# A two-layer diffusion trunk: twelve modulation vectors as row sums, spread over the whole program

## The chip, the cores and the metric

The kernel runs on one core of a Trainium2 chip. TensorE (PE) multiplies, VectorE (DVE), ScalarE (ACT) and GpSimd (POOL) work on rows of 128 partitions, and SyncE (SP) issues most transfers. Each engine takes its instructions in the order in which they are written, and waits on semaphores of the others. The metric is the device time in microseconds (us), lower is better.

## The reference, cut to what matters

```python
for l in range(2):                                 # two layers, same weights for context and latent tokens
    mods = split(silu(cond) @ w_ada[l] + b_ada[l], 9)      # shift, scale, gate of three norms; 1024 each
    x += 0.5 * gt1 * swiglu(rms_norm(x, g0) * (1 + sc1) + sh1)      # ffn1, 1024 -> 2*2816 -> 1024
    u = rms_norm(x, g1) * (1 + sc2) + sh2
    z = u @ w_in                                   # 1024 -> 4112: attention, Fourier, mLSTM, gates
    x += gt2 * ((sum over 3 branches of sigmoid(u @ w_gate_b) * (branch_b @ w_br_b)) @ w_out)
    x += 0.5 * gt3 * swiglu(rms_norm(x, g2) * (1 + sc3) + sh3)      # ffn2
y = rms_norm(x, g_final)
```

There are 128 context and 128 latent tokens, so 256 columns. Everything is float32. `cond` is one vector for the context tokens and one for the latent ones, so that each of the 9 modulations of a layer is a product of a 1024 x 1024 matrix with two columns.

## The kernel before, in words

The tokens lie as columns: `xT` holds 8 blocks of 128 channels by 256 tokens. The products take a float32 weight as two parts, a rounded high half (`whi`, cast on ACT) and the rest (`wlo`, subtracted on DVE); activations are split the same way (`uh`, `ul`), and `mm3` does three products for each pair. A weight arrives by DMA in chunks of up to 1 MB into one of 6 `raw` buffers, is split in units of 128 x 1024 elements by `split_one`, and up to 6 units may be split and not yet used up.

The program is a list of steps. `add` appends a step with its function and the units that it needs; the last loop walks over the list, calls each function, and behind most steps `pump_split` splits further units while fewer than 6 are live. The order of that walk is the order of each engine's queue. A unit that isn't split (`split=False`) is read straight from `raw`.

A layer is FFN 1, mixer and FFN 2. An FFN has an input stage (11 pairs of 4 units of 24 products, `silu` times gate) and an output stage (4 pairs of output blocks, 3 units for each block, then `residual` adds into `xT`). The mixer projects `w_in`, and then runs three branches with their gates; pieces of attention and of the recurrence (`lanes`) are run between and within its steps. `w_out` ends it. In the attention, DVE makes `pc` (the difference of two softmaxes) and PE transposes it.

Layer 0 starts with `begin`: in 9 slices PE makes the first shift and scale (`ada`, one block of 128 channels each), `channel` turns it into `uh`, `ul`, and `products` runs three FFN pairs, each slab of whose weights is one channel block deep. Three pairs of PSUM tiles are evicted at its end by `done`.

The other 16 modulations (the dictionary `ADA`) are made either on DVE (first list of an entry: a product with the condition `cb` along rows of the transposed weights `w_adaT`, with the sum kept; 16 of these sums make one modulation) or on PE (second list: raw weights against `cT`, in two groups of 16 products each, copied to `adaev` and transposed at the end). `mod_steps` writes both, and `spread_into` spreads them evenly over a stage: the whole FFN input stage or the mixer's branches.

Of the kernel before, what the change touches and what calls it, by code (L numbers as in the profile page):

```python
# [116 lines left out]
class Step:  # L117
    def __init__(self, fn, units=(), pump=True, lanes=False, ahead=()):
        self.fn, self.units, self.pump, self.lanes = fn, list(units), pump, lanes
        self.ahead = list(ahead)  # L120


@with_exitstack
def trunk_kernel(ctx: ExitStack, tc: tile.TileContext, a: dict):
# [94 lines left out]
    run = {"lanes": False}  # L219
    late, held = [], []  # L220

    def add(fn, units=(), pump=True, ln=False, ahead=()):
        steps.append(Step(fn, units, pump, ln, ahead))

    def pump_lanes(which=(0, 1, 2)):
# [69 lines left out]


    def mod_steps(mods_):

        on_ve, mods_ = mods_
        st = {"left": 4 * len(mods_)}
        seq = []

# [10 lines left out]

        def finish(l, m, o, x):
            bT = parT[l][:, m * KD:(m + 1) * KD].unsqueeze(2).to_broadcast([P, KD, 2])
            ve.tensor_add(o, x, bT)  # L320
            if m % 3 == 1:
                k0 = 72 + m // 3 * KD
                gT = parT[l][:, k0:k0 + KD].unsqueeze(2).to_broadcast([P, KD, 2])
                ve.scalar_tensor_tensor(o, o, 1.0, gT, op0=ALU.add, op1=ALU.mult)
            elif m % 3 == 2 and m != 5:
                ve.tensor_scalar(o, o, 0.5, None, op0=ALU.mult)

        for i, (l, m) in enumerate(on_ve):
            o, junk = mods[l, m], []
            for j in range(KD // 2):  # L330
                ch = Chunk(a["w_adaT"][l, m, j], 2, D)
                for b in range(2):
                    for g in range(2):
                        u = Unit(ch, b, b + 1, 0, D, split=False)

                        def fn(u=u, k=2 * j + b, g=g, o=o, l=l, m=m, junk=junk):
                            if not junk:
                                junk.append(blk([P, D], "junkw"))
                            ve.tensor_tensor_reduce(junk[0], u.raw()[:, 0, :], cb[:, g, :], 1.0, 0.0,  # L339
                                                    op0=ALU.mult, op1=ALU.add, accum_out=o[:, k, g:g + 1])  # L340
                            if k == KD - 1 and g == 1:
                                finish(l, m, o, o)

                        seq.append(((i + (4 * j + 2 * b + g) / 16) / len(on_ve), fn, [u]))
        for i, (l, m) in enumerate(mods_):
            for j2 in range(2):
                us = []
                for j in range(2 * j2, 2 * j2 + 2):
                    ch = Chunk(a["w_ada"][l, j * 256:(j + 1) * 256, m * D:(m + 1) * D], 2, D)
                    us.append(Unit(ch, 0, 2, 0, D, split=False))  # L350

                def fn(us=us, i=i, j2=j2):
                    for j, u in enumerate(us, 2 * j2):
                        raw = u.raw().rearrange("p e (r c f) -> p e c r f", r=2, c=2)
                        side([(cT[:, 2 * j + e, CT - 2 * i:CT - 2 * i + 32], raw[:, e, c])
                              for e in range(2) for c in range(2)], 0, 512)

                seq.append(((2 * i + j2 + 0.4) / (2 * len(mods_)), fn, us))
        seq.sort(key=lambda x: x[0])
        out = [x[1:] for x in seq]  # L360
        if not mods_:
            return out

        def post():
# [12 lines left out]
            for i, (l, m) in enumerate(mods_):  # L377
                finish(l, m, mods[l, m], full[:, :, 2 * i:2 * i + 2])

        out.append((post, []))  # L380
# [174 lines left out]

    def residual(k, ps, gate, norm):
        for g in range(2):
# [25 lines left out]
    def add_ffn(l, which, norm, norm_next, mods_, begun=None):  # L583
        w_out = a[f"w_ffn{which}_out"][l]
        gate = mods[l, 2 if which == 1 else 8]
        hT = {}

# [28 lines left out]
        n_pair = NF // 2  # L616
        p0 = len(steps)
        for jj in range(n_pair):
            if jj == FIRST + 1 and l == 0 and which == 1:
                add(s_params2)  # L620
            if jj == 0:
                if begun is not None:
# [4 lines left out]
            elif begun is None or jj >= FIRST:  # L627
                us, st = ffn_units(l, which, jj), {}
                for nm, i in (("a", 0), ("a", 1), ("g", 0), ("g", 1)):
# [12 lines left out]
                    add(fn, [us[2 * i + (nm == "g")]])  # L642
        p1 = len(steps)

        ks = [(0, 8), (8, 16), (16, 22)]
        for mp in range(4):
            ps = [None, None]
            for k0, k1 in ks:
                ch = Chunk(w_out[k0 * P:k1 * P, mp * 256:(mp + 1) * 256], k1 - k0, 256)
                for i in range(2):  # L650
# [3 lines left out]
                    def fn(u=u, i=i, m=m, ps=ps, k0=k0, k1=k1):  # L654
# [6 lines left out]
                        if k1 == NF:  # L661
                            residual(m, ps[i], gate, norm_next)

                    add(fn, [u], pump=not (mp == 3 and k1 == NF))
        spread_into(p0 + (14 if begun else 0), p1, mods_)


    def add_mixer(l, norm, norm_next, mods_):
# [522 lines left out]

        us = b8_units(w_in, 0) + b8_units(w_in, 256)
        add(lambda: first(norm, us, q_done), us, pump=2)
        add(loads2, pump=False)
        bform("k", 512)
        aform("v", 1024, v_tile)
        steps.insert(len(steps) - 3, Step(gates))
# [6 lines left out]

        p0 = len(steps) + 6
        mg = {}
        wb = {0: a["w_br_attn"][l], 1: a["w_br_four"][l], 2: a["w_br_mlstm"][l]}
        wg = a["w_branch_gate"][l]
        for bi, br in enumerate(BRANCHES):
            for mq in range(2):  # L1210
# [14 lines left out]
                if mq == 0:  # L1225
                    def drain(br=br):
                        while not M.get(f"ok{br}") and pump_lanes():
                            pass
                    add(drain)

                for p in range(2):
                    def fb(u=Unit(chb, 0, 4, p * 256, p * 256 + 256), st=sts[p], p=p, mq=mq, bi=bi, br=br):
# [30 lines left out]

        gate = mods[l, 5]
        for mp in range(4):
            us_ = b8_units(a["w_out"][l], mp * 256)
            if mp == 0:
                def fn(us_=us_):
# [6 lines left out]
                    for m in range(2):  # L1275
                        residual(m, ps[m], gate, norm_next)
                add(fn, us_)
                continue
            for i in range(2):
                def fn(u=us_[i], m=2 * mp + i):  # L1280
                    p_ = pm([P, 256])
                    prod8(p_, u, mk_)
                    residual(m, p_, gate, norm_next)
                add(fn, [us_[i]], pump=mp < 3)
        spread_into(p0, len(steps) - 8, mods_)
        return loads
# [16 lines left out]
    def begin(done):  # L1303
# [5 lines left out]
        win = a["w_ffn1_in"][0]  # L1309
        ev, ps, v = {}, [], []  # L1310
        b1 = tmp([P, KD], "b1", bufs=1)
# [21 lines left out]
        def channel(k):  # L1333
# [26 lines left out]
        def slice_(j, u, us):  # L1360
            if j < KD:
                ada(j, u)
            if j == 0:
# [41 lines left out]
    for l in range(DEPTH):  # L1405
        add_ffn(l, 1, norms[l, 0], norms[l, 1], ADA[l, "ffn1"], begin if l == 0 else None)
        pos = len(steps)
        steps.insert(pos - 6, Step(add_mixer(l, norms[l, 1], norms[l, 2], ADA[l, "mixer"]), pump=False))
        add_ffn(l, 2, norms[l, 2], norms[l + 1, 0], ADA[l, "ffn2"])

# [17 lines left out]

    add(fin)


# [113 lines left out]
```

## Time and profile before

| | us |
|---|---|
| median of three runs | 1352.44 (1351.43 to 1352.7) |
| the profiled execution | 1352.04 |
| its span, first to last instruction | 1350.3 |
| PE, DVE, ACT, POOL busy in the span | 1325.8, 961.0, 683.5, 112.4 |

The execution's own time is 1.7 us longer than its span. Busy time is time in which at least one instruction of the engine runs; an engine that is always busy need not be the one that sets the time, so waits are read beside it.

### The profile page before, as it was taken

Reading aid. Unit: us, or ns where it says so; the run is one execution under the profiler, and the core shown is the slowest. Engines: PE = TensorE matmul, PEld = TensorE weight load, DVE = VectorE, ACT = ScalarE, POOL = GpSimd, SP = SyncE. Lnnn points to the kernel's source line nnn. Section 1 sums busy time; section 2 is a strip of 40 time slices with the busy share of each in tenths; the row PEclk is TensorE's granted clock in tenths of the full one; section 3 lists DMA queues with packets and bytes.
Section 4 is the critical chain, followed back from the end, with each engine's and each line's share of the span. In section 5 each row is a group of like instructions: output and inputs, shape, how many; then the busy total and the mean of one; then the engine's idle time right before and its main releaser. Section 6 shows DMA issues by size and latency. Waiting matters only on the chain.

```text
span 1350.3 us, 25902 instructions
## 1 busy us (share of the span) xinstructions
PE 1325.8 (98%) x10748; PEld 1257.2 (93%) x10748; DVE 961.0 (71%) x1535; ACT 683.5 (51%) x1097; POOL 112.4 (8%) x136
## 2 busy tenths in 40 slices
PE   8999999999999999999999999999999999999998
PEld 5899999788989998999999999998899899999998
DVE  4699866775557689977669976677565668886653
ACT  4564445665644465444455444456654445654441
POOL 2000003100000040000120000130000001200001
PEclk9999999999999999999999999999999999999999
DMA  9999864754588638987639886747446895477630
GB/s 366 339 342 320 289 191 148 219 183 129 172 287 304 221 126 282 312 303 234 197 125 304 305 297 201 200 146 218 132 152 226 294 303 163 153 259 236 216 100 32
DMA packets 220565, 304.72 MB, mean 226 GB/s; under 512 B 5584, under 2 KB 190176, under 8 KB 215712
## 3 DMA queue, kind: packets, MB, share of 16 engines
q1 hardware_dynamic: 216320, 295.93, 65.8%
q0 software_dynamic: 1680, 5.05, 1.1%
q10 hardware_dynamic: 2448, 2.10, 0.6%
q8 instruction: 84, 1.38, 0.4%
q14 instruction: 33, 0.27, 0.1%
HBM read 298.85 MB, written 3.15 MB: 224 GB/s over the span
## 4 chain that ended last, share of the span: by engine, by line
PE 83%; DVE 9%; ACT 3%; DMA 3%; issue 2%; ACTq 0%; POOL 0%; SPq 0%; DVEq 0%
PE pm L167 24%; PE pm L169 24%; PE pm L168 24%; PE pd L164 3%; DVE wlo L1474 3%; PE pb L164 2%; ACT whi L1473 2%; DVE v L488 2%; DMA raw<-w_ada 2%; DVE ul L179 1%; DVE junkw L339 1%; PE pa L164 1%; PE pm L736 1%; PE pm L738 1%; PE pm L737 1%
## 5 line engine op out<-in xcount | busy, mean ns | idle before, releaser
L1474 DVE TENSOR_TENSOR wlo<-raw,whi 128x1024 fp32r<-128x1024 f32 (+1 forms) x428 | 508.9, 1195 | 282.9 <-ACT whi L1473 275.2
L1473 ACT CAST whi<-raw 128x1024 fp32r<-128x1024 f32 (+1 forms) x428 | 434.9, 1025 | 336.3 <-PE pm L168 242.2
L167 PE MATMUL pm<-uh,whi 128*128 128x256 f32 x1904 | 545.2, 286 | 1.9 <-ACT uh L178 1.0
L169 PE MATMUL pm<-uh,wlo 128*128 128x256 f32 x1904 | 536.0, 282 | 4.9 <-DVE wlo L1474 4.9
L168 PE MATMUL pm<-ul,whi 128*128 128x256 f32 x1904 | 536.5, 282 | 1.8 <-DVE v L488 1.3
L167 PEld LDWEIGHTS pm<-uh,whi 128*128 128x128 f32 x1904 | 360.5, 189 | 20.9 <-issue 8.8
L169 PEld LDWEIGHTS pm<-uh,wlo 128*128 128x128 f32 x1904 | 358.8, 188 | 6.4 <-DVE wlo L1474 6.3
L168 PEld LDWEIGHTS pm<-ul,whi 128*128 128x128 f32 x1904 | 359.8, 189 | 4.3 <-DVE ul L179 1.9
L169 PE MATMUL pm<-hh,wlo 128*128 128x256 f32 x704 | 198.3, 282 | 0.0
L168 PE MATMUL pm<-hl,whi 128*128 128x256 f32 x704 | 197.8, 281 | 0.0
L167 PE MATMUL pm<-hh,whi 128*128 128x256 f32 x704 | 197.6, 281 | 0.0
L339 DVE CUSTOM_DVE_ANT_0 junkw<-raw,cb 128x1024 f32<-128x1024 f32 x112 | 136.5, 1219 | 0.1
L167 PEld LDWEIGHTS pm<-hh,whi 128*128 128x128 f32 x704 | 132.8, 189 | 0.0
L168 PEld LDWEIGHTS pm<-hl,whi 128*128 128x128 f32 x704 | 132.7, 188 | 0.0
L169 PEld LDWEIGHTS pm<-hh,wlo 128*128 128x128 f32 x704 | 132.5, 188 | 0.0
L413 POOL TENSOR_TENSOR nsum<-nsum,nsq 128x256 f32<-128x256 f32 x36 | 36.4, 1011 | 806.5 <-ACT nsq L411 806.5
L637 ACT ACTIVATE silu<-pm 128x512 f32<-128x512 f32 x38 | 22.7, 597 | 53.1 <-PE pm L169 53.1
L164 PE MATMUL pd<-raw,cT 128*32 128x512 f32 (+1 forms) x416 | 43.8, 533 | 4.9 <-DMA raw<-w_ada 4.9
L178 ACT CAST hh<-silu 128x512 fp32r<-128x512 f32 x41 | 25.3, 621 | 37.6 <-DVE silu L639 37.6
L558 DVE SCALAR_TENSOR_TENSOR xT<-pm,mod,xT 128x128 f32<-128x128 f32 x96 | 28.8, 342 | 17.9 <-PE pm L169 17.8
L1222 ACT ACTIVATE sig<-pm 128x512 f32<-128x512 f32 x24 | 14.4, 598 | 49.9 <-PE pm L169 49.8
L736 PE MATMUL pm<-whi,uh 128*128 128x512 f32 x96 | 39.3, 410 | 0.0
(337 smaller groups left out, 1755.5 us busy)
## 6 DMA issues: line engine op xcount, KB each, us to landing
raw<-w_ffn_in SPq DMA_DIRECT2D x82, 1024.0 KB, 7.1
raw<-w_ada SPq DMA_DIRECT2D x44, 1024.0 KB, 5.6
raw<-w_ffn_out SPq DMA_DIRECT2D x32, 1024.0 KB, 5.6
raw<-w_in SPq DMA_DIRECT2D x32, 1024.0 KB, 5.8
raw<-w_adaT SPq DMA_DIRECT2D x28, 1024.0 KB, 6.5
raw<-w_branch_gate SPq DMA_DIRECT2D x24, 1024.0 KB, 5.3
raw<-w_ffn_out SPq DMA_DIRECT2D x16, 768.0 KB, 4.6
raw<-w_out SPq DMA_DIRECT2D x8, 1024.0 KB, 6.3
```

The costliest lines, as they stand in the source:

```text
L164: pe.matmul(out, lhsT, rhs, start=start, stop=stop)
L167: pe.matmul(out, sh, mh, start=start, stop=False)
L168: pe.matmul(out, sh, ml, start=False, stop=False)
L169: pe.matmul(out, sl, mh, start=False, stop=stop)
L178: ac.copy(hi, src)
L339: ve.tensor_tensor_reduce(junk[0], u.raw()[:, 0, :], cb[:, g, :], 1.0, 0.0, op0=ALU.mult, op1=ALU.add, accum_out=o[:, k, g:g + 1])
L413: eng.tensor_add(self.sum, self.sum, sq)
L488: ve.tensor_scalar(v[:, G[1]], v[:, G[1]], self.scale[:, k, 1:2], self.shift[:, k, 1:2], op0=ALU.mult, op1=ALU.add)
L558: ve.scalar_tensor_tensor(xT[:, k, G[g]], ps[:, G[g]], gate[:, k, g:g + 1], xT[:, k, G[g]], op0=ALU.mult, op1=ALU.add)
L736: pe.matmul(ps[g], xh[:, G[g]], wh, start=(k == 0), stop=False)
L1473: ac.copy(u.hi, r)
L1474: ve.tensor_sub(u.lo, r, u.hi.bitcast(F32))
```

## The change

Of the 16 modulations behind `begin`, 12 are now row sums on DVE instead of 7, and 4 stay on PE instead of 9 (`ADA`, one for each of four stages). The 192 row sums (12 times 16) stand in one list in the order of `ROWS`, and no longer belong to a stage: each step of the program has a rate (`RATE`: 0.93 or 0.85 for a step of an FFN's input stage, 0.75 in the output stage except its last quarter, 0.3 in the mixer's projections, 0.35 and 0.5 in its branches, 0 elsewhere), and whenever the rates of the steps passed add up to one, the next sum is put behind that step. The product that a sum leaves behind goes to one bf16 tile, `junkw`, instead of a float32 block.

In `begin`, POOL no longer multiplies `xT` by the norm's factor ahead of the channels; each channel now does that with its scale in two DVE operations, adds the shift in the cast on ACT, and subtracts in two more DVE operations. In the first slice, the channel comes ahead of both splits of the slab. In the last slice, one split stands ahead of each of the three evictions.

```diff
-CT = 8
-
-ADA = {(0, "ffn1"): ([(0, 4), (0, 3)], [(0, 2)]),
-       (0, "mixer"): ([], [(0, 7), (0, 6), (0, 5)]),
-       (0, "ffn2"): ([(1, 1), (1, 0)], [(0, 8)]),
-       (1, "ffn1"): ([(1, 4), (1, 3)], [(1, 2)]),
-       (1, "mixer"): ([], [(1, 7), (1, 6), (1, 5)]),
-       (1, "ffn2"): ([(1, 8)], [])}
+CT = 0
+
+ADA = {(0, "ffn1"): [(0, 2)], (0, "mixer"): [(0, 5)], (0, "ffn2"): [(0, 8)], (1, "mixer"): [(1, 5)]}
+ROWS = [(0, 4), (0, 3), (0, 7), (0, 6), (1, 1), (1, 0), (1, 2), (1, 4), (1, 3), (1, 7), (1, 6), (1, 8)]
+
+RATE = {"in0": 0.93, "in": 0.85, "out": 0.75, "win": 0.3, "branch": 0.35, "last": 0.5, "merge": 0.0}
...
+    junkw = const.tile([P, D], BF16, name="junkw")
...
+    def row_steps():
+
+        for l, m in ROWS:
+            o = mods[l, m]
+            for j in range(KD // 2):
+                ch = Chunk(a["w_adaT"][l, m, j], 2, D)
+                for b in range(2):
+                    for g in range(2):
+                        u = Unit(ch, b, b + 1, 0, D, split=False)
+
+                        def fn(u=u, k=2 * j + b, g=g, o=o, l=l, m=m):
+                            ve.tensor_tensor_reduce(junkw, u.raw()[:, 0, :], cb[:, g, :], 1.0, 0.0,
+                                                    op0=ALU.mult, op1=ALU.add, accum_out=o[:, k, g:g + 1])
+                            if k == KD - 1 and g == 1:
+                                finish(l, m, o, o)
+                                known.add((l, m))
+
+                        yield fn, [u]
...
-            i, r = k // 4, k % 4
-            x = v[i][:, r, :]
-            ac.activation(x[:, G[0]], x[:, G[0]], AF.Identity, scale=sc[:, 0:1], bias=sh[:, 0:1])
-            ve.tensor_scalar(x[:, G[1]], x[:, G[1]], sc[:, 1:2], sh[:, 1:2], op0=ALU.mult, op1=ALU.add)
-            hilo(x, U.h[i][:, r, :], U.l[i][:, r, :])
+            x = t2([P, 256], "v0")
+            xh, xl = uk(k)
+            for g in range(2):
+                ve.scalar_tensor_tensor(x[:, G[g]], xT[:, k, G[g]], sc[:, g:g + 1], norm.bc[:, G[g]],
+                                        op0=ALU.mult, op1=ALU.mult)
+            for g in range(2):
+                ac.activation(xh[:, G[g]], x[:, G[g]], AF.Identity, bias=sh[:, g:g + 1])
+            for g in range(2):
+                ve.scalar_tensor_tensor(xl[:, G[g]], x[:, G[g]], sh[:, g:g + 1], xh[:, G[g]].bitcast(F32),
+                                        op0=ALU.add, op1=ALU.subtract)
...
-                for i in range(2):
-                    v.append(blk([P, 4, 256], f"v{i}"))
-                    for r in range(4):
-                        (po if i or r else ve).tensor_mul(v[i][:, r, :], xT[:, 4 * i + r, :], norm.bc)
...
             if j < KD:
-                split_one()
+                if j:
+                    split_one()
                 channel(j)
-                split_one()
+                while st["unit"] < 2 * j + 2:
+                    split_one()
             else:
+                pump_split(1)
                 done(0, ps[0])
             for i in range(1, FIRST):
                 if j:
                     products(j - 1, i, us)
                 if j == KD:
+                    pump_split(1)
                     done(i, ps[i])
...
+    todo, due = row_steps(), 0.0
+    for s in steps:
+        s.slot = []
+        due += s.rate
+        while due >= 1.0:
+            due -= 1.0
+            nxt = next(todo, None)
+            if nxt is not None:
+                s.slot.append(Step(*nxt))
+    steps[:] = [x for s in steps for x in (s, *s.slot)]
```

Three places of DVE's queue show what moves. The first is the first channel of `begin`; `mo` is the channel's modulation as summed from PSUM, `v` the normed block. Before:

```order
L1373 TENSOR_TENSOR v_213<-xT,bcs 128x256
L1474 TENSOR_TENSOR wlo<-raw_122,whi 128x768
L1340 TENSOR_REDUCE mo_230<-pd 128x4
L1343 SCALAR_TENSOR_TENSOR mod_1_97<-mo_230,b_119,parT_94 128x2
L1344 TENSOR_SCALAR mod_0_96<-mo_230,parT_94 128x2
L1348 TENSOR_SCALAR v_213<-v_213,mod_1_97,mod_0_96 128x128
L179 TENSOR_TENSOR ul_201<-v_213,uh_199 128x256
L1474 TENSOR_TENSOR wlo<-raw_122,whi 128x768
```

And in the changed kernel, where the slab's two splits (`wlo`) come behind the channel:

```order
L1359 TENSOR_REDUCE mo_217<-pd 128x4
L1362 SCALAR_TENSOR_TENSOR mod_1_97<-mo_217,b_120,parT_94 128x2
L1363 TENSOR_SCALAR mod_0_96<-mo_217,parT_94 128x2
L1367 SCALAR_TENSOR_TENSOR v_221<-xT,mod_1_97,bcs 128x128 x2
L1372 SCALAR_TENSOR_TENSOR ul_202<-v_221,mod_0_96,uh_200 128x128 x2
L1510 TENSOR_TENSOR wlo<-raw_123,whi 128x768 x2
```

The second place is the output stage of layer 0's first FFN, the first unit of `w_out` behind two residuals (`xT`), before:

```order
L558 SCALAR_TENSOR_TENSOR xT<-pm,mod_2_98,xT 128x128 x2
L1474 TENSOR_TENSOR wlo<-raw_1790,whi 128x768
L426 TENSOR_SCALAR y<-xT,mod_4_100 128x128
L179 TENSOR_TENSOR yl_2083<-y,yh_2081 128x256
L1474 TENSOR_TENSOR wlo<-raw_1855,whi 128x1024 x2
L1474 TENSOR_TENSOR wlo<-raw_1859,whi 128x1024 x2
L558 SCALAR_TENSOR_TENSOR xT<-pm,mod_2_98,xT 128x128 x2
```

And now, where `junkw` marks a row sum (the row behind it reads the sum out):

```order
L559 SCALAR_TENSOR_TENSOR xT<-pm,mod_2_98,xT 128x128 x2
L1510 TENSOR_TENSOR wlo<-raw_1877,whi 128x768
L426 TENSOR_SCALAR y<-xT,mod_4_100 128x128
L178 TENSOR_TENSOR yl_2097<-y,yh_2095 128x256
L319 ISA junkw,mod_7_103<-raw_1874,cb 128x1024
L319 ISA mod_7_103 128x1
L1510 TENSOR_TENSOR wlo<-raw_1940,whi 128x1024 x2
L319 ISA junkw,mod_7_103<-raw_1874,cb 128x1024
L319 ISA mod_7_103 128x1
L1510 TENSOR_TENSOR wlo<-raw_2004,whi 128x1024
```

Between two residuals stand four or five sums that were not there. Counted over the program, the output stages of the four FFNs now hold 19, 18, 19 and 0 sums (4, 3, 3 and 2 before), the input stages 25, 29, 29 and 11 (28, 29, 29 and 14 before), each mixer 21 (none before).

The third place is the mixer of layer 0, from the row maxima `mx` of the attention scores to `pc`. The rows on `gpk` are the gates of the recurrence. Before:

```order
L1474 TENSOR_TENSOR wlo<-raw_2847,whi 128x1024 x2
L835 TENSOR_REDUCE mx<-pa 128x4 x2
...
L1474 TENSOR_TENSOR wlo<-raw_2892,whi 128x1024
L844 RECIPROCAL rs<-sm 128x8
L846 TENSOR_TENSOR cf<-sm,rs 128x4
L847 TENSOR_SCALAR cf<-cf,lamn 128x4
L849 SCALAR_TENSOR_TENSOR pc<-e_3192,cf,pc 128x128 x4
```

And now, with one sum between the two splits ahead of `mx` and one behind the last split ahead of `pc`:

```order
L1510 TENSOR_TENSOR wlo<-raw_2878,whi 128x1024
L319 ISA junkw,mod_7_103<-raw_2888,cb 128x1024
L319 ISA mod_7_103 128x1
L1510 TENSOR_TENSOR wlo<-raw_2878,whi 128x1024
L845 TENSOR_REDUCE mx<-pa 128x4 x2
...
L1510 TENSOR_TENSOR wlo<-raw_3003,whi 128x1024
L319 ISA junkw,mod_7_103<-raw_2888,cb 128x1024
L319 ISA mod_7_103 128x1
L854 RECIPROCAL rs<-sm 128x8
L856 TENSOR_TENSOR cf<-sm,rs 128x4
L857 TENSOR_SCALAR cf<-cf,lamn 128x4
L859 SCALAR_TENSOR_TENSOR pc<-e_3224,cf,pc 128x128 x4
```

In layer 1 two sums stand in the same stretch, the second one split earlier.

## Rows read from the trace of the kernel before

**Rows 1.** The page's busy time (share of the span) and instructions of each engine.

```profile
PE 1325.8 (98%) x10748; PEld 1257.2 (93%) x10748; DVE 961.0 (71%) x1535; ACT 683.5 (51%) x1097; POOL 112.4 (8%) x136
```

**Rows 2.** The list of waits: who waited for whom, us in total, times, longest.

```profile
ACT whi L1473 <- PE pm L168: 242.2, 165, 4.3
...
PE pm L169 <- DVE wlo L1474: 4.9, 7, 0.8
```

**Rows 3.** PE's timeline around one group: start, us, operation, count.

```profile
129.22 0.28 PE L169 MATMUL pm<-uh,wlo 128*128 128x256 f32 x1
129.43 1.92 PE L164 MATMUL pd<-raw,cT 128*32 128x512 f32 x16
131.28 0.39 PE L167 MATMUL pm<-uh,whi 128*128 128x256 f32 x1
131.51 0.28 PE L168 MATMUL pm<-ul,whi 128*128 128x256 f32 x1
```

**Rows 4.** PE's timeline at a closing step of layer 1's mixer.

```profile
1112.76 0.60 PE L172 MATMUL pd<-cst,adaev 128*128 128x128 f32 x4
1113.11 0.36 PE L167 MATMUL pm<-uh,whi 128*128 128x256 f32 x1
```

**Rows 5.** PE's timeline in FFN 1 of layer 1, and PE's waits from 60 us.

```profile
725.65 1.07 PE L164 MATMUL pd<-raw,cT 128*32 128x512 f32 x8 [1.41 <-DMA raw<-w_ada]
...
PE pd L164 <- DMA raw<-w_ada: 2.7, 3, 1.4
```

**Rows 6.** PE's timeline at the end of the opening, idle time before it in brackets.

```profile
63.01 0.38 PE L167 MATMUL pm<-uh,whi 128*128 128x256 f32 x1 [0.91 <-ACT whi L1473]
...
64.27 0.39 PE L169 MATMUL pm<-uh,wlo 128*128 128x256 f32 x1 [0.76 <-DVE wlo L1474]
```

**Rows 7.** PE's timeline around the first slab's products.

```profile
14.30 1.07 PE L164 MATMUL pd<-raw,cT 128*32 128x256 f32 x16 [1.16 <-DMA raw<-w_ada]
16.41 0.38 PE L167 MATMUL pm<-uh,whi 128*128 128x256 f32 x1 [1.04 <-ACT uh L178]
18.28 0.39 PE L169 MATMUL pm<-uh,wlo 128*128 128x256 f32 x1 [0.32 <-DVE wlo L1474]
```

**Rows 8.** DVE's timeline in the first channel and in the second.

```profile
12.73 1.09 DVE L1474 TENSOR_TENSOR wlo<-raw,whi 128x768 fp32r<-128x768 f32 x1 [0.31 <-ACT whi L1473]
...
14.34 0.78 DVE L1344 TENSOR_SCALAR mod<-mo,parT 128x2 f32<-128x2 f32 x1
15.16 0.70 DVE L1348 TENSOR_SCALAR v<-v,mod,mod 128x128 f32<-128x128 f32 x1
...
20.08 0.22 DVE L1344 TENSOR_SCALAR mod<-mo,parT 128x2 f32<-128x2 f32 x1
20.41 0.34 DVE L1348 TENSOR_SCALAR v<-v,mod,mod 128x128 f32<-128x128 f32 x1
```

**Rows 9.** POOL's timeline in the first slice.

```profile
12.04 6.79 POOL L1373 TENSOR_TENSOR v<-xT,bcs 128x256 f32<-128x256 f32 x7 [2.02 <-ACT bcs L476]
```

**Rows 10.** Four stretches: length, busy PE, PEld, DVE, ACT, POOL, clock, DMA.

```profile
18.40:22.00 3.60, 3.60 (x18) 3.60 (x19) 2.55 (x6) 1.57 (x3) 0.43 (x1) 0.53 1.03 419
28.00:34.00 6.00, 6.00 (x59) 5.28 (x58) 3.13 (x7) 3.04 (x7) 0.00 (x0) 1.00 0.93 341
157.00:222.00 65.00, 65.00 (x550) 65.00 (x549) 39.88 (x64) 29.93 (x43) 5.75 (x6) 1.00 0.66 204
260.00:440.00 180.00, 178.39 (x1363) 160.27 (x1362) 113.06 (x195) 95.78 (x189) 8.79 (x11) 1.00 0.64 214
```

**Rows 11.** DVE's timeline at the first row sum, with what follows it.

```profile
73.20 1.22 DVE L339 CUSTOM_DVE_ANT_0 junkw<-raw,cb 128x1024 f32<-128x1024 f32 x1
74.34 0.09 DVE L339 DVE_READ_ACCUMULATOR2_ANT mod<- 128x1 f32 x1
74.34 1.22 DVE L1474 TENSOR_TENSOR wlo<-raw,whi 128x1024 fp32r<-128x1024 f32 x1
```

**Rows 12.** The mixer of layer 0: DVE's timeline, and PE's transposes of `pc`.

```profile
270.57 1.23 DVE L1474 TENSOR_TENSOR wlo<-raw,whi 128x1024 fp32r<-128x1024 f32 x1 [0.90 <-ACT whi L1473]
...
282.53 1.14 DVE L849 SCALAR_TENSOR_TENSOR pc<-e,cf,pc 128x128 f32<-128x128 f32 x4
...
282.94 1.11 PE L172 MATMUL pa<-cst,pc 128*128 128x128 f32 x4 [0.52 <-DVE pc L849]
```

More of the change, by code (lines that the diff above doesn't have):

```diff
@@ L120, in __init__ @@
         self.ahead = list(ahead)
+        self.rate = 0.0
 @with_exitstack
@@ L218, in trunk_kernel @@
     lanes = [[], [], []]
-    run = {"lanes": False}
+    run = {"lanes": False, "rate": 0.0}
     late, held = [], []
@@ L223, in add @@
         steps.append(Step(fn, units, pump, ln, ahead))
+        steps[-1].rate = run["rate"]
     def pump_lanes(which=(0, 1, 2)):
@@ L294, in x_in, with finish @@
                 (ac.copy if g and not k4 else ve.tensor_copy)(xT[:, 4 * k4:4 * k4 + 4, G[g]], t)
+    def finish(l, m, o, x):
+        bT = parT[l][:, m * KD:(m + 1) * KD].unsqueeze(2).to_broadcast([P, KD, 2])
+        ve.tensor_add(o, x, bT)
+        if m % 3 == 1:
+            k0 = 72 + m // 3 * KD
+            gT = parT[l][:, k0:k0 + KD].unsqueeze(2).to_broadcast([P, KD, 2])
+            ve.scalar_tensor_tensor(o, o, 1.0, gT, op0=ALU.add, op1=ALU.mult)
+        elif m % 3 == 2 and m != 5:
+            ve.tensor_scalar(o, o, 0.5, None, op0=ALU.mult)
+    def row_steps():
[13 more added lines that the diff above has]
+                        yield fn, [u]
+    known = set()
     def mod_steps(mods_):
-        on_ve, mods_ = mods_
         st = {"left": 4 * len(mods_)}
-        seq = []
+        out = []
         def side(tiles, f0, f1):
@@ L316, in side @@
                 ac.copy(st["ev"], st["ps"])
[L318 to L344, printed above, removed]
         for i, (l, m) in enumerate(mods_):
@@ L356, in fn @@
                               for e in range(2) for c in range(2)], 0, 512)
[L358 to L362, printed above, removed]
+                out.append((fn, us))
         def post():
@@ L378, in post @@
                 finish(l, m, mods[l, m], full[:, :, 2 * i:2 * i + 2])
+                known.add((l, m))
         out.append((post, []))
@@ L554, in prod8, with residual @@
                 mid()
-    def residual(k, ps, gate, norm):
+    def residual(k, ps, gate, norm, of):
+        assert of <= known, (of, known)
         for g in range(2):
@@ L585, in add_ffn @@
         gate = mods[l, 2 if which == 1 else 8]
+        of = {(l, 2), (l, 3), (l, 4)} if which == 1 else {(l, 8), (l + 1, 0), (l + 1, 1)}
+        of = {x for x in of if x[0] < DEPTH}
         hT = {}
@@ L617, in add_ffn @@
         p0 = len(steps)
+        run["rate"] = 0.0
         for jj in range(n_pair):
@@ L620, in add_ffn @@
                 add(s_params2)
+            if jj == (FIRST if begun else 1):
+                run["rate"] = RATE["in0" if begun else "in"]
             if jj == 0:
@@ L643, in add_ffn @@
         p1 = len(steps)
+        run["rate"] = RATE["out"]
         ks = [(0, 8), (8, 16), (16, 22)]
@@ L647, in add_ffn @@
             ps = [None, None]
+            if mp == 3:
+                run["rate"] = 0.0
             for k0, k1 in ks:
@@ L661, in fn @@
                         if k1 == NF:
-                            residual(m, ps[i], gate, norm_next)
+                            residual(m, ps[i], gate, norm_next, of)
                     add(fn, [u], pump=not (mp == 3 and k1 == NF))
-        spread_into(p0 + (14 if begun else 0), p1, mods_)
+        if mods_:
+            spread_into(p0 + (14 if begun else 0), p1, mods_)
     def add_mixer(l, norm, norm_next, mods_):
@@ L1192, in add_mixer @@
         us = b8_units(w_in, 0) + b8_units(w_in, 256)
+        run["rate"] = 0.0
         add(lambda: first(norm, us, q_done), us, pump=2)
@@ L1195, in add_mixer @@
         bform("k", 512)
+        run["rate"] = RATE["win"]
         aform("v", 1024, v_tile)
@@ L1205, in add_mixer @@
         p0 = len(steps) + 6
+        run["rate"] = RATE["branch"]
         mg = {}
@@ L1228, in drain @@
                             pass
+                    if bi == 2:
+                        run["rate"] = RATE["last"]
                     add(drain)
+                if bi == 2 and mq == 1:
+                    run["rate"] = 0.0
                 for p in range(2):
@@ L1262, in mk_ @@
             return mg["h", k // 4][:, k % 4, :], mg["l", k // 4][:, k % 4, :]
-        gate = mods[l, 5]
+        gate, of = mods[l, 5], {(l, 5), (l, 6), (l, 7)}
         for mp in range(4):
             us_ = b8_units(a["w_out"][l], mp * 256)
+            run["rate"] = RATE["merge"] if mp in (1, 2) else 0.0
             if mp == 0:
@@ L1275, in fn @@
                     for m in range(2):
-                        residual(m, ps[m], gate, norm_next)
+                        residual(m, ps[m], gate, norm_next, of)
                 add(fn, us_)
@@ L1282, in fn @@
                     prod8(p_, u, mk_)
-                    residual(m, p_, gate, norm_next)
+                    residual(m, p_, gate, norm_next, of)
                 add(fn, [us_[i]], pump=mp < 3)
-        spread_into(p0, len(steps) - 8, mods_)
+        if mods_:
+            spread_into(p0, len(steps) - 8, mods_)
         return loads
@@ L1429, in trunk_kernel @@
     add(fin)
+    todo, due = row_steps(), 0.0
[8 more added lines that the diff above has]
+    steps[:] = [x for s in steps for x in (s, *s.slot)]
+    assert next(todo, None) is None
     units, need, floor = [], {}, 0
```

8 lines of the change are left out of this document (4 added, 4 removed).

## The prediction

> **What bounds the kernel now.** I read the page's busy table first: TensorE (PE) is busy in 98% of the 1350.3 us span, VectorE (DVE) in 71%, ScalarE (ACT) in 51% [rows 1]. A busy PE need not be the bound, so the list of waits comes next. The reader should see its direction: ACT waits 242.2 us for PE to give back a buffer of split weights, and PE waits only 4.9 us for the low halves that DVE makes [rows 2]. So the two engines that prepare the weights run their full six splits ahead nearly all the time, and PE sets the pace. What leaves PE's queue shortens the program; what is added on DVE costs nothing as long as DVE keeps its lead, and what it delays is not a thing that PE takes next.
>
> **The change, part by part**
>
> *Five modulations leave PE.* Each has two groups of 16 products. Around one group, product starts stand 129.22 to 131.28, and the next gap is 0.23 where 0.12 is usual [rows 3]. So a group costs 2.06 - 0.12 + 0.11 = 2.05 us; ten groups: 20.5 us. One closing step of five goes as well: four transposes of 0.60 us in the trace's busy time, but the next product starts 0.35 us after them [rows 4]; I take 0.4. Nothing hides either: PE's rows touch on both sides.
>
> *Waits for the weights of those groups.* The stall before the second half of the group at 723 us is 1.41 us, and this group is gone; three such stalls sum to 2.7 us [rows 5]. The other two belong to groups that stay but move; 0 to 1.3 us, I take half, 0.6. Together 2.0.
>
> *Splits amid the first evictions.* After the nine-step opening PE idles 0.91 us for the first high half and 0.76 us for its low half [rows 6], because ACT and DVE evict three pairs before they split. Now a split stands before each eviction, some 3 us ahead of PE's need. Gain 0 to 1.67; I take 1.7. Later evictions are the price: the PSUM buffers that they free are next written by PE after the pair that it is then on, so one split's delay is hidden.
>
> *First channel.* The second half of the first slab is waited for until 18.28 us; the first product had waited until 16.41, behind a group that itself waited for its DMA until 14.30 [rows 7]. In the DVE queue a split of 1.09 us stands ahead of the channel's small operations, and two of these take 0.78 and 0.70 us where the next channel takes 0.22 and 0.34, while POOL runs its products [rows 8, 9]. Now the split comes behind, and POOL is idle: 1.09 + 0.56 + 0.36 = 2.0 us earlier. The DMA limits it: if PE ran straight on from 14.30 + 1.07 = 15.37, the ninth product would start at 15.37 + 8 x 0.12 = 16.3 instead of 18.28. I take 1.9; bounds 0 and 2.0. Each channel's DVE work becomes four short two-input operations in place of one and a subtraction; this is hidden under PE's own slice, in which DVE is busy 3.13 us of 6 [rows 10]. If the clock's slow stretch behind it, 3.60 us at 0.53 (the lower level) [rows 10], also went, up to 1.5 us more would be gained; PE still stops for the same DMA before it, so I count 0.
>
> *Eighty more row sums on DVE.* One takes 1.22 us, and the next operation starts 1.14 us after it, the read of the sum lying beside it [rows 11]. In the three FFN output stages 19, 18 and 19 stand where 4, 3 and 3 stood, in the two mixers 21 each where none stood; the FFN input stages have 6 fewer and the last output stage 2. The first output stage keeps DVE busy 39.88 of 65 us [rows 10], its few old sums included; 15 more make 39.9 + 17.1 = 57.0. It fits, with a lead of six splits before it and none of the sums in its last quarter, so 0. The mixer of layer 0 keeps DVE busy 113 of 180 us [rows 10], and 21 sums add 24. Room again, but here order matters: two sums now stand ahead of the attention operation that writes `pc`, and PE waits for just this one already, 0.52 us at 282.94 [rows 12]. The first sum falls partly into the 0.90 us for which DVE idles at 270.57; the second falls into a stretch without a gap [rows 12]. So `pc` comes 0.24 + 1.14 = 1.4 us later, and PE with it; the same in layer 1: -2.8 us. Bounds 0 and two full sums, 4.6. What is queued behind on DVE (gate rows, a split) has waited for other things than PE. For the other 38 mixer sums the trace shows no PE wait that they would lengthen; each could cost nothing or up to 1.14 us. I take 1.0 us for all, nearest to a stretch in which PE has hardly any idle.
>
> Does a sum really cost 1.22 us in its new place? It writes bf16 now, and no such sum ran before; the copied-out product is never read, and every sum before took two f32 inputs at the pace of a plain subtraction of equal length, 1.22 us [rows 11].
> [...]
>
> Sum: 20.5 + 0.4 + 2.0 + 1.7 + 1.9 - 2.8 - 1.0 = 22.7 us. The profiled execution took 1352.04 us, 1.7 more than its span; the median of the runs is 1352.44. From the former 1329.3, from the latter 1329.7, which I give.
>
> **The rivals**
>
> 1. *The sums reach PE.* If one in four of the other 38 mixer sums stood before something that PE takes next, and each output stage lost one sum's length at its end, 10 x 1.14 + 3 x 1.14 = 15 us would be lost, less the 1.0 already counted: 1343. For it: two of 42 clearly do. Against it: DVE idle before most splits, ACT's long waits for PE.
> 2. *The gain runs into the lead.* PE, relieved, catches up with the splits and waits there: if half of the 20.5 came back, 1340. Against it: 242.2 us of ACT waiting for PE, some twelve times what is removed.
> 3. *Slower: the mixer's chain.* The attention and recurrence operations pass from PE to DVE and back; if most mixer sums stood in that chain, up to 38 x 1.14 = 43 us would be lost, at the full count 1329.7 + 42 = 1372. It decides from 21 of the 38 on (23.7 us against 22.7 + 1.0). Against it: PE waited for DVE in this chain only at `pc`.
> 4. *Dearer sums.* The output stage has (65 - 39.9)/15 = 1.67 us for each added sum; at twice the measured length, 2.44 us, it would overrun by 11.6 us, and three of them bring 35 us: 1365, slower. The measured 1.22 leaves it little chance. [...]
> 5. *Better.* `pc` and the other mixer sums cost nothing, the slow-clock stretch and all DMA stalls go: 1329.7 - 2.8 - 1.0 - 1.5 - 0.7 = 1323.7.
>
> **How the numbers follow.** Chances: forecast (1325 to 1336) 0.66, rival 1 0.18, rival 2 0.05, rival 3 0.03, rival 4 0.02, better 0.06. A measurement of this kernel tells about 0.2%, some 2.7 us, from no change. The range goes from 1322, just past the better case, to 1339, which cuts off most of rivals 1 and 2, 3 and 4: 0.8 are inside. Faster 0.94 (all but rivals 3, 4 and a sliver of 1), within 0.2% 0.02, slower 0.04.
>
> **What would show it.** Right: PE busy near 1301 us; about 21 us fewer PE products; no gap at 62 us; first slab's ninth product near 16.4; PE's wait for `pc` near 1.9 us in each mixer; row sums of 1.22 us; ACT still waiting over 200 us for PE. Wrong: PE waits for low halves grow by more than a few us (output stages or rival 2), waits for attention or state tiles spread through the mixers (1 or 3), sums above 1.6 us (4), or a first product still after 16 us (first channel).

## The result, and the profile after

The changed kernel takes 1339.53 us (median of four runs, 1338.31 to 1340.78) against 1352.57 of the kernel before: a ratio of 0.9903 (95% interval 0.9885 to 0.9920), faster by 13.0 us. Forecast were 1329.7 us, 1322 to 1339: the direction is right, the time lies half a microsecond outside the range, and of the forecast gain of 22.7 us 57% came.

The page of the changed kernel, its first busy line:

```profile
span 1339.0 us, 25750 instructions
PE 1310.1 (98%) x10584; PEld 1257.7 (94%) x10584; DVE 1048.9 (78%) x1707; ACT 678.8 (51%) x1096; POOL 105.3 (8%) x129
```

Against [rows 1] PE's busy time fell by 15.7 us, not to the 1301 that I had named; DVE's rose by 87.9. The list of waits, in the columns of [rows 2]:

```profile
PE pd L163 <- DMA raw<-w_ada: 6.7, 4, 3.4
PE pm L167 <- DVE v L488: 3.5, 2, 2.8
PE pa L171 <- DVE pc L859: 3.5, 2, 1.8
PE pm L168 <- DVE wlo L1510: 3.2, 5, 0.8
PE pb L171 <- DVE ha L1178: 1.6, 2, 0.9
```

PE waits no more than before for low halves (4.9 then), so the sums did not eat the lead of the splits. What has grown is the wait for the modulations' own weights (`w_ada`, 4.9 before), for the normalised `v` (1.3 before) and for `pc` (1.0 before); that for `ha` is new, and that for `kctx` (1.3 before) is gone.

Where did the gain go on the way? ACT's first operation on a finished product is a milestone of PE; where no idle time stands ahead of it, ACT had other work just before and may be late by some tenths of a microsecond. Four such milestones, first of the changed kernel, then of the kernel before (start, duration, operation; in brackets the idle time ahead):

```profile
148.94 0.60 ACT L643 ACTIVATE silu<-pm 128x512 f32<-128x512 f32 x1 [1.87 <-PE pm L168]
346.51 0.60 ACT L1235 ACTIVATE sig<-pm 128x512 f32<-128x512 f32 x1
506.94 0.59 ACT L643 ACTIVATE silu<-pm 128x512 f32<-128x512 f32 x1
534.06 0.60 ACT L643 ACTIVATE silu<-pm 128x512 f32<-128x512 f32 x1 [8.25 <-PE pm L168]
```

```profile
154.31 0.60 ACT L637 ACTIVATE silu<-pm 128x512 f32<-128x512 f32 x1 [1.86 <-PE pm L169]
348.30 0.60 ACT L1222 ACTIVATE sig<-pm 128x512 f32<-128x512 f32 x1
515.41 0.59 ACT L637 ACTIVATE silu<-pm 128x512 f32<-128x512 f32 x1
535.93 0.60 ACT L637 ACTIVATE silu<-pm 128x512 f32<-128x512 f32 x1 [0.51 <-PE pm L169]
```

The difference of the two starts is the lead of the changed kernel. Taken at each stage's mark in the same way:

| from mark to mark | lead at its end | gained or lost |
|---|---|---|
| start to the last `silu` of FFN 1, layer 0 | 5.4 | +5.4 |
| to the mixer's first `sig` (FFN output, mixer's input stage) | 1.8 | -3.6 |
| to FFN 2's first `silu` (four groups gone) | 8.5 | +6.7 |
| to its third `silu` | 1.9 | -6.6 |
| to its last | 1.0 | -0.9 |
| to the last `silu` of FFN 1, layer 1 (two groups gone) | 7.5 | +6.5 |
| to that mixer's first `sig` | 4.0 | -3.5 |
| to FFN 2's first `silu` (four groups gone) | 11.6 | +7.5 |
| to the end | 11.3 | -0.3 |

Three places lose: both mixer fronts (the stretch from the end of FFN 1 to the mixer's first `sig`) and, most, the 27 us after FFN 2's first `silu` in layer 0. PE's timeline there:

```profile
521.35 0.28 PE L168 MATMUL pm<-uh,wlo 128*128 128x256 f32 x1
523.69 1.07 PE L163 MATMUL pd<-raw,cT 128*32 128x512 f32 x8 [2.05 <-DMA raw<-w_ada]
528.20 1.94 PE L163 MATMUL pd<-raw,cT 128*32 128x512 f32 x8 [3.45 <-DMA raw<-w_ada]
530.06 0.58 PE L166 MATMUL pm<-uh,whi 128*128 128x256 f32 x1
```

The first of this modulation's two groups, a group that stayed on PE, now waits 2.05 us for its first half and 3.45 for its second; in the kernel before it waited 0.80 in all:

```profile
528.96 1.07 PE L164 MATMUL pd<-raw,cT 128*32 128x512 f32 x8 [0.80 <-DMA raw<-w_ada]
```

The second half now takes 1.94 us in place of 1.07. The stretches of the changed kernel say why (length, busy PE, PEld, DVE, ACT, POOL, granted clock, DMA):

```profile
515.00:520.00 5.00, 5.00 (x44) 5.00 (x44) 5.00 (x8) 3.93 (x5) 0.00 (x0) 1.00 0.87 264
520.00:525.00 5.00, 2.70 (x22) 1.59 (x21) 5.00 (x8) 0.75 (x2) 0.00 (x0) 1.00 0.92 323
525.00:530.00 5.00, 1.80 (x8) 0.20 (x8) 4.38 (x7) 0.81 (x1) 0.00 (x0) 0.52 0.93 317
530.00:535.00 5.00, 5.00 (x38) 4.94 (x35) 0.00 (x0) 0.94 (x2) 0.00 (x0) 0.80 1.07 383
```

The granted clock, 1.00 until 525, fell while PE stood from 524.8 to 528.2: in windows of 1 us it was 0.60 from 525 and 0.50 from 526 to 532. The group's first half took 1.07 us at 1.00, its second 1.94 at 0.50. DVE has no gap from 515 to 525, and from 520 on ACT hardly works. SP queued the two transfers at 516.79 and 520.22, and what it had waited for from 505 to 531 us was mostly DVE, 21.0 of 25.4 us:

```profile
SPq L1490 <- DVE wlo L1510: 10.2, 3, 3.6
SPq L1490 <- DVE hl L178: 5.9, 1, 5.9
SPq L1490 <- DVE mod L319: 4.9, 2, 3.5
```

SP's own rows, first of the changed kernel, then of the kernel before, show two things more:

```profile
506.95 4.46 SPq L1490 DMA_DIRECT2D raw<-w_ffn_in  x2
515.05 0.34 SPq L1490 DMA_DIRECT2D raw<-w_adaT  x1
516.79 3.79 SPq L1490 DMA_DIRECT2D raw<-w_ada  x2
```

```profile
509.43 6.35 SPq L1454 DMA_DIRECT2D raw<-w_ffn_in  x2
520.64 3.79 SPq L1454 DMA_DIRECT2D raw<-w_ada  x2
```

The stage holds 29 row sums in both kernels, but the group now stands later in it: PE was ready for its first half 14.7 us after the start of the first `silu`, 11.7 before. From that `silu` on SP now queues three transfers ahead of the group's (two of `w_ffn_in`, one of `w_adaT`) where one stood before (at 515.41, the second of its row), and each waits for a buffer. And the group's two transfers were longer on their way: PE went on 6.9 and 8.0 us after they were queued, while they had landed after 5.1 and 4.9 us before; the DMA engines are at 0.87 and 0.92 from 515 to 525 us, against 0.64 and 0.62 in the kernel before:

```profile
515.00:520.00 5.00, 5.00 (x45) 5.00 (x44) 5.00 (x9) 3.84 (x5) 0.00 (x0) 1.00 0.64 209
520.00:525.00 5.00, 5.00 (x44) 5.00 (x44) 5.00 (x8) 0.33 (x1) 0.00 (x0) 1.00 0.62 207
```

### The profile page after: what moved, and what is told of

Read it like the earlier page. It is cut to its first block, busy times and chain, and to the rows that moved or that the text cites. A ratio compares the mean times of both kernels' runs of the same rounds, so it can differ in the third digit from the quotient of the medians.

```text
span 1339.0 us, 25750 instructions
## 1 busy us (share of the span) xinstructions
PE 1310.1 (98%) x10584; PEld 1257.7 (94%) x10584; DVE 1048.9 (78%) x1707; ACT 678.8 (51%) x1096; POOL 105.3 (8%) x129
## 4 chain that ended last, share of the span: by engine, by line
PE 81%; DVE 11%; ACT 3%; issue 2%; DMA 2%; ACTq 0%; POOL 0%; SPq 0%; DVEq 0%; POOLq 0%
PE pm L166 24%; PE pm L168 24%; PE pm L167 23%; DVE wlo L1510 3%; PE pb L163 2%; PE pd L163 2%; DVE v L488 2%; ACT whi L1509 2%; DMA raw<-w_ada 1%; DVE ul L178 1%; PE pm L746 1%; PE pm L748 1%; PE pm L747 1%; PE pa L163 1%; DVE junkw L319 1%
## 5 line engine op out<-in xcount | busy, mean ns | idle before, releaser
L1509 ACT CAST whi<-raw 128x1024 fp32r<-128x1024 f32 (+1 forms) x428 | 434.4, 1024 | 297.7 <-PE pm L167 213.8
L319 DVE CUSTOM_DVE_ANT_0 junkw<-raw,cb 128x1024 bf16<-128x1024 f32 x192 | 233.8, 1218 | 0.0
L411 ACT ACTIVATE nsq<-xT 128x256 f32<-128x256 f32 x42 | 17.5, 418 | 53.3 <-DVE xT L559 53.2
L747 PE MATMUL pm<-wlo,uh 128*128 128x512 f32 x96 | 37.9, 394 | 0.0
```

What stands on the lines that cost most here:

```text
L319: ve.tensor_tensor_reduce(junkw, u.raw()[:, 0, :], cb[:, g, :], 1.0, 0.0, op0=ALU.mult, op1=ALU.add, accum_out=o[:, k, g:g + 1])
L747: pe.matmul(ps[g], xh[:, G[g]], wl, start=False, stop=False)
L1509: ac.copy(u.hi, r)
```

## Experiments

Ratios are to the kernel before on the same chip; 0.001 is 1.35 us.

**e1: the modulation's weights queued earlier.**

```diff
-            at = max(floor, len(units) - N_SPLIT) if u.split else len(units)
+            at = max(floor, len(units) - N_SPLIT) if u.split or u.soon else len(units)
...
                     us.append(Unit(ch, 0, 2, 0, D, split=False))
+                    us[-1].soon = True
```

> The changed kernel, with one thing altered: the DMA of a modulation's weights (w_ada) is queued as early as that of weights that are to be split, so two to four transfers sooner on SP's queue. Queue theory: in the second FFN of layer 0 the two waits for w_ada (2.05 and 3.45 us at 523.69 and 528.20 in the changed kernel) go, and with them the stretch at the lower clock behind them (granted clock 0.52 in 525 to 530, 0.80 in the next five); some 8 us less, 1331 to 1333. Rival (DVE is full there, the sums delay the low halves and so the raw buffers): the transfer only changes places, PE then waits for a high or low half in the same stretch, 1337 to 1341. Second rival (the clock falls for another reason): the waits go, the low clock stays, about 1334.

Measured: 1334.86 us, 0.9862 (0.9848 to 0.9875). The waits are gone, and the clock is full in the same stretches:

```profile
520.00:525.00 5.00, 5.00 (x43) 3.43 (x42) 4.53 (x6) 2.91 (x4) 0.00 (x0) 1.00 1.03 375
525.00:530.00 5.00, 5.00 (x44) 5.00 (x43) 5.00 (x8) 2.64 (x4) 0.00 (x0) 1.00 1.09 362
```

From FFN 2's first to its third `silu` the lead over the kernel before grows by 0.9 us where the change lost 6.6: 7.5 us are regained there. The median gained less, 5.5 us by the ratios. The traces are of single executions, the change's of the slowest of its four and e1's of the fastest; and the two waits together vary where nothing at this place was altered (5.3 us in e3 and e9, 3.4 in e5, 3.0 in e12). One wait for `ha` (1.80 us at 1046.82) is new in e1's trace.

**e2: short sums.** `tensor_tensor_reduce` reads `[:, 0:64]` of its 1024 columns, so most of each sum is left out; nothing else differs.

> The changed kernel with each row sum over 64 of its 1024 columns (the modulations are therefore wrong; transfers, raw buffers and the order of every instruction stay). A sum should take about 0.15 us in place of 1.22, DVE busy falls by some 200 us to about 845. If DVE's time is what makes the w_ada transfers late, their waits in the second FFN go with the low clock, and the waits for pc (1.69 and 1.76) and ha (0.69 and 0.87) too: 1324 to 1329. If the order on SP's queue and the holding of raw buffers do it, the w_ada waits stay at 4 to 6 us and only pc and ha go: 1333 to 1337. If neither counts, 1338 to 1341.

Measured: 1328.66 us, 0.9815 (0.9802 to 0.9829). A sum takes 219 ns and DVE is busy 870.1 us. The wait for `w_ada` at that place is 1.42 us once in place of 5.50, and the eight products behind it take 1.06 us (the row below); PE's waits for `pc` are 0.70 and 0.62, and none for `ha` is left. So DVE's time made much of the delay: of SP's waiting from 505 to 531 us in the changed kernel, 21.0 of 25.4 us were for DVE. But all 192 sums are shortened here, the 112 old ones too, so the run doesn't show what the 80 new ones alone did; and changing the order on the queue alone (e1) also cures it. Neither pure theory holds, and how much of the 5.50 us is DVE's time, the place in the queue or the longer way of the transfers was not taken apart: here too PE went on with the second half only 7.8 us after its transfer was queued (at 511.35):

```profile
519.19 1.06 PE L163 MATMUL pd<-raw,cT 128*32 128x512 f32 x8 [1.42 <-DMA raw<-w_ada]
```

**e3: no sum ahead of `pc`.** The mixer's first rate starts at `mk`, doubled, instead of at `v`.

> The changed kernel, with the row sums of each mixer's input stage put into its last twelve steps, so that none stands ahead of the operation that writes pc. My term of 1.4 us a mixer: PE's waits for pc fall from 1.69 and 1.76 to about 0.5, and the low clock behind the first (0.72 in 280 to 285) goes: 1335.5 to 1337. Rival (the sums are only pushed into the next link of the chain): a wait of like size for another attention or state tile, 1338 to 1341.

Measured: 1335.44 us, 0.9868 (0.9855 to 0.9882). PE waits 0.55 and 0.47 us for `pc` as before the change, and the low clock at 280 to 285 (0.72 in the changed kernel) is gone. At 4.7 us by the ratios the gain is nearly twice the 2.4 us of the waits. Between the marks around the fronts 3.3 us are regained in layer 0, where low clock followed the stop in the changed kernel, and 1.6 in layer 1, where none did (1.00 from 940 to 950): there the wait is nearly the whole loss. Not all of the 3.3 us need be the sums' doing: the changed kernel's clock was also lower at 235 to 245, ahead of `pc` (0.51 and 0.81; 0.66 and 1.00 in e3), and in e1, with a wait of 1.86 us for the first `pc`, it stayed at 1.00 behind it. The wait for `w_ada` in FFN 2 is unchanged (1.86 and 3.46).

**e4: the opening alone, and e12: all but the opening.** The change's edits in `begin`, `channel` and `step` put into the kernel before (e4), or taken back out of the changed one (e12).

> The kernel before with the changed opening alone (first channel's operations and the splits amid the first evictions); modulations as before. My two terms, 1.9 and 1.7: 1349. By the progress of PE in the changed kernel's trace (5.4 us ahead at the tenth silu of the first FFN, low clock in the opening gone): 1347. Rival (the lead gained in the opening is lost at the next stage's front, where PE waits for the normalisation anyway): 1351 to 1353.

> The changed kernel with the opening of the kernel before; the row sums as changed. If the opening's gain (0.9959 alone) and that of the row sums add: 0.9903 + 0.0041 = 0.9944, about 1345.5 on this chip. If the opening's gain is what lets the sums' losses show (PE arrives earlier at the transfers it waits for), less than that is lost: 0.991 to 0.993.

Measured: e4 1348.12 us, 0.9959 (0.9947 to 0.9972); e12 1345.45 us, 0.9944 (0.9932 to 0.9956). They add to the change's 0.9903, so the opening is worth 5.5 us and the modulations 7.6. In e4's trace PE's last product of the nine steps starts at 59.02 instead of 61.82, and the fourth one behind it, past the two gaps of [rows 6], at 59.49 instead of 64.49: a lead of 2.8, then of 5.0 us.

**e5: GpSimd's set-up two steps later, and e8: the same with e1 and e3.** `loads2` moved behind two steps of `bform("k")`.

> The changed kernel, with GpSimd's set-up of each mixer (the transfers of caches and state, the clearing of two tiles) issued two steps later, behind the products that read v. In the changed kernel DVE's v operations stand for 2.14 and 4.33 us while POOL issues these, and PE waits 0.64 and 2.83 us for them, with a stretch at the lower clock behind each. If POOL's set-up holds DVE up: both waits go, and the low clock behind them, 3 to 6 us less, 1334 to 1337. If it holds up whatever DVE does then, low halves come late two steps later and PE waits there as long: 1338 to 1341. If the v operations are slow for another reason (the row sums ahead), the waits stay.

> The two edits of the run before and GpSimd's set-up two steps later as well. If the waits for v are POOL's doing and their clock stretch goes with them: 3 to 6 us below that run, 1324 to 1327, and with the prediction's own figure (1329.7) passed. If the hold-up only moves: as the run before, 1329 to 1331.

Measured: e5 1340.74 us, 0.9909 (0.9892 to 0.9925); e8 1331.98 us, 0.9843 (0.9828 to 0.9857), no different from e7 below. The edit did not do what it was for: in the trace the set-up still stands right behind POOL's last multiplication (883.73, then 884.72), because POOL's queue waits for nothing between. These two runs say nothing on the waits for `v`.

**e6 and e10: PE kept busy through the wait.** Products that nothing reads stand ahead of the waiting ones (the edit is e10's):

```diff
+                        if (l, m, j2) == (0, 8, 0):
+                            t = pb([P, 2, P])
+                            for _ in range(18 + 12 * j):
+                                mm(t, identb, maskb)
```

> The changed kernel, with 18 and 30 products of 256 columns, read by nothing, queued on PE ahead of the two groups of the second FFN's modulation in layer 0, which wait for w_ada 2.05 and 3.45 us. They fill the wait and shorten nothing. If the low clock behind (0.52, then 0.80) comes of PE standing still, it stays at full, and about 3 us are gained: 1336 to 1337.5. If the clock falls for another reason, or the filling products delay the groups, 1339 to 1342.

> The changed kernel with products that nothing reads where PE really waits: 18 ahead of the first eight and 30 ahead of the second eight products of the first group of the second FFN's modulation in layer 0 (in the run before, the 30 stood ahead of the second group, where PE did not wait, and cost their 3.45 us). If the low clock comes of PE's standing still there, the clock stays near full in 520 to 535 and about 2 to 3 us are gained while the transfers land as late as before: 1337 to 1338.5. If the clock falls all the same, 1340 to 1342.

Measured: e6 1341.12 us, 0.9910 (0.9895 to 0.9925); e10 1337.01 us, 0.9882 (0.9867 to 0.9896). In e6 I had misread the two waits as those of two groups; the 30 products stood at 558 us, where PE did not wait. In e10 the clock stays at 1.00 from 520 to 535, the second half of the group takes 1.07 us instead of 1.94, and with transfers no earlier the loss between the first and third `silu` is 4.6 us instead of 6.6. So 2 us of that loss went with the low clock; the medians differ by 2.8 us.

**e7: e1 and e3 together.**

> The changed kernel with both edits tried one at a time before: w_ada queued as early as weights to be split, and no row sum ahead of pc. Alone they gave 0.9862 and 0.9868 of the kernel before, against 0.9903. If the two losses are independent, the gains add: 0.983, about 1330. If they share a cause (one clock stretch, DVE's lead), only the larger shows: 1334 to 1335.

Measured: 1330.88 us, 0.9836 (0.9821 to 0.9851): two independent losses, which add within the intervals (0.9827 if in full).

**e9 and e11: GpSimd's set-up off GpSimd.** In `loads2`, `po.dma_start` becomes a transfer of ScalarE's queue, `po.memset` becomes `ve.memset`; e11 adds e1 and e3.

> The changed kernel, with the mixer's set-up taken off GpSimd: the three transfers are issued by ScalarE, the two tiles cleared by DVE behind the v operations. (Moving the set-up by two steps had left it in its place, since POOL's queue waits for nothing there.) If POOL's set-up is what makes DVE's v operations stand for 2.14 and 4.33 us: they take 0.34, PE's waits for v (0.64 and 2.83) go, and with them part of the low clock behind: 1335 to 1338. If the v operations are slow by themselves there: waits as before, 1339 to 1342, the two clearings on DVE a loss of up to 1 us each. If ScalarE's issuing takes the place: PE waits for high halves or uh there, 1339 to 1342.

> The two edits that added up (w_ada queued earlier, no row sum ahead of pc) with the set-up taken off GpSimd. If the set-up is the cause of the waits for v: 2 to 5 us below the two edits' 0.9836, so 0.980 to 0.982, 1326 to 1329. If not, 0.983 to 0.985.

Measured: e9 1344.98 us, 0.9940 (0.9927 to 0.9953); e11 1335.81 us, 0.9873 (0.9861 to 0.9886). The waits for `v` (0.64 and 2.83 us in the changed kernel) are gone, but the transfer of the cache is issued 10 us later (239.34 for 229.60), behind ScalarE's work, and PE waits for it 4.94 and 4.77 us in e9: that GpSimd's set-up makes the waits is shown, but this cure was worse.

**e13 and e14: on top of e7, the clearing alone; and early transfers.** e13 changes the two `po.memset` to `ve.memset`; e14 also issues the three transfers from ScalarE ahead of the mixer's `first`.

> The two edits that added up (w_ada queued earlier, no row sum ahead of pc; 0.9836 of the kernel before) and the two tiles of the mixer's set-up cleared by DVE, behind the v operations, in place of GpSimd; GpSimd still issues the three transfers. If the clearing is what holds DVE in layer 1 (its v operation stands for 4.33 us there, until GpSimd's clearing ends, but 2.14 in layer 0, until its last transfer is issued): 2.14 in both layers, PE's wait for v 0.65 in both, 2 to 3 us less: 0.981 to 0.982. If the issuing alone holds it: 2.83 stays, 0.983 to 0.985.

> As the run before, and the three transfers issued by ScalarE ahead of the mixer's normalisation. If GpSimd's set-up is the whole cause of the waits for v: none are left in either layer, DVE's v operations take 0.34 us, no wait for the cache, and the clock behind stays higher: 3 to 6 us below 0.9836, so 0.979 to 0.981. If the fronts are slow for other reasons (low halves, the clock falling anyway): 0.982 to 0.985. If the early transfers crowd out the weights' transfers there: above 0.985.

Measured: e13 1329.62 us, 0.9826 (0.9811 to 0.9841); e14 1328.86 us, 0.9817 (0.9804 to 0.9831). First DVE and POOL in layer 1 of the changed kernel, then of e13:

```profile
887.56 4.33 DVE L488 TENSOR_SCALAR v<-v,mod,mod 128x128 f32<-128x128 f32 x1
888.73 0.89 POOL L692 DMA_DIRECT2D C<-state_C  x1
889.62 0.81 POOL L694 MEMSET zgh<- 128x832 f32 x1
890.35 0.81 POOL L695 MEMSET zgl<- 128x832 f32 x1
891.58 0.22 POOL L1000 MEMSET g<- 36x128 f32 x1
```

```profile
876.88 0.60 DVE L490 TENSOR_SCALAR v<-v,mod,mod 128x128 f32<-128x128 f32 x1
877.49 0.62 DVE L490 TENSOR_SCALAR v<-v,mod,mod 128x128 f32<-128x128 f32 x1
878.04 0.89 POOL L694 DMA_DIRECT2D C<-state_C  x1
878.93 0.33 POOL L1000 MEMSET gpk<- 40x256 f32 x1
```

A `v` operation that stood from 887.56 to 891.89, until POOL's last clearing was over, takes 0.60 us without the two large ones, and PE's waits for `v` are gone in both layers, that of 0.64 in layer 0 too, which I had expected to stay. In layer 1 the lead between the last `silu` of FFN 1 and the mixer's first `sig`, which fell by 3.5 us in the changed kernel and 1.9 in e7, grows by 0.3. Part comes back: PE then waits 2.22 us for the attention's `kctx`, in e14 in both layers. By time alone e7, e13 and e14 cannot be told apart; all three intervals lie wholly below the change's, and e14 has the lowest median of those that leave nothing out.

## Why the prediction came out short

- **Groups off PE (20.5 + 0.4): right.** Two groups, one stall of 1.41 and a closing step should give 5.9 us in FFN 1 of layer 1; its marks from first to last `silu` give 7.48 - 1.74 = 5.7. The mixers' marks from first to last `sig`, 7.3 and 7.6, and the waits for `ha` in them, 0.69 and 0.87, make 8.0 and 8.5 for four groups at 2.05 (8.2).
- **"The other two belong to groups that stay but move; 0 to 1.3 us, I take half": the step that failed.** I had only seen how those stalls could end. One did (0.48 us at 85.64; it is gone in e4 too, where no group moved); the other grew from 0.80 to 5.50 us, and the clock fell to 0.50 with it: 7.5 us by e1's trace, 5.5 by its median. Sums and splits whose time I had found to fit on DVE hold the raw buffers in which this group's weights must land, and the move put two more transfers ahead of them. I costed DVE's time against PE's need for low halves, never against SP's need for buffers.
- **`pc` (2.8): right as a wait, too small as a loss.** The waits grew by 1.2 and 1.3 us; 4.7 came back when the sums were moved (e3). The rest came back in layer 0 with the low clock (0.72), which did not follow such a wait in every trace (1.00 in e1, e5 and e10).
- **Missing: `v` in layer 1.** 0.65 became 2.83 us, with a stretch at 0.50 of the clock behind it. I had no term for it; the sums' length has no part in it (2.86 in e2), POOL's clearing has (no wait for `v` is left in e13). It came with the edits to the modulations (2.90 in e12, 0.73 with the opening alone in e4); which of them makes DVE's operation stand 4.33 us in layer 1 where it stood 2.14 before was not found.
- **Opening (1.9 + 1.7 = 3.6): right in place, measured 5.5.** The ninth product starts 1.5 us earlier, 16.75 for 18.28, not 1.9: my 15.37 for a first product took the group's start from the old trace, and it now waited for its DMA until 14.70. But the low clock of [rows 10], which I had left in because PE would stop for this DMA, went all the same (1.00 from 15 to 25 us, in e4 too), and the second group starts 3.1 us earlier:

```profile
14.70 1.07 PE L163 MATMUL pd<-raw,cT 128*32 128x256 f32 x16 [0.97 <-DMA raw<-w_ada]
16.75 0.35 PE L168 MATMUL pm<-uh,wlo 128*128 128x256 f32 x1
20.43 1.07 PE L163 MATMUL pd<-raw,cT 128*32 128x256 f32 x16
```

```profile
23.56 1.07 PE L164 MATMUL pd<-raw,cT 128*32 128x256 f32 x16
```

  The splits amid the evictions gave 2.2 instead of 1.7: from start to start of products the two gaps of [rows 6] are 1.19 and 1.04 us, with 0.22 to the next start behind each, where 0.12 is usual, more than the idle time in the rows.
- **Other 38 mixer sums (1.0): 1.9.** `ha` 0.69 and 0.87, `xT` 0.34 us; none of the three is left in e2.
- **Output stages (0) and a sum of 1.22 us: right.** From 66 to 232 us, the first output stage included, the trace shows no wait of PE. All 192 sums, which write bf16, take 1210 to 1222 ns, the 112 of the kernel before, which wrote float32, 1215 to 1225; none came near the 2.44 us of *Dearer sums*.

The rivals: 1340 (the gain runs into the lead) hit the number by a mechanism that did not occur, for PE's waits for low halves fell. *The sums reach PE* was nearer, but by way of a transfer rather than of attention tiles. With both losses that e1 and e3 remove, the change gives 1330.9, within 1.2 us of the forecast. That closeness is partly luck: the opening's surplus of 1.9 us stands against the 2.2 us by which the wait for `v` grew.

## What to carry to other kernels

Work added to an engine with time to spare must be checked against all that waits for this engine: here not the matrix products but the DMA queue, which gets its buffers back from it. Work that moves must be checked against the transfers that are then queued ahead of its own. A transfer that is needed unsplit should be queued as far ahead as the others. And a stop of PE can cost more than its length: here, with the clock at 0.50 from 526 to 532 us, 2 us on top of 5.5 by e10.

## What the runs showed of the hardware

- **POOL's clearing held DVE here.** A DVE operation of 0.34 us stood 4.33 us beside transfers issued and tiles cleared by POOL, longer than any one of POOL's instructions beside it (0.22 to 0.89); with the large clearings gone it took 0.60 (e13), with the issuing gone too 0.34 in layer 0 (e14) and 0.45 in layer 1 (e9 and e14). Why the same code held DVE for 2.14 us in layer 0, from 230.00 to 232.14 and so for the most part before the clearing began at 232.05, was not found.
- **The clock after short stops is not settled.** Behind the front of layer 0's mixer, with waits of about 0.65 and 0.5 to 0.8 us each time, it was 1.00 in e4 and e7, 0.66 for one stretch of 5 us in e1 and 0.51 in the changed kernel. Between the same two marks e1's trace loses 1.5 us where the changed kernel's loses 3.6, with waits for `pc` as long. Behind the first wait for `pc` the clock fell to 0.70 to 0.73 for 5 us in the changed kernel, e6, e9 and e12 (waits of 1.69 to 1.83 us), and stayed at 1.00 in e1, e5 and e10 (1.85 and 1.86 us).
